# Attention units and projection passes: the second head pair's gates kept in DRAM until they are used, and a new spread of passes over the units

## The chip, the cores and the metric

The kernel runs on one core of one Trainium2 chip. The metric is the device time of one execution in microseconds (us). The core has a matrix engine (TensorE, PE; its weight loads are shown apart as PEld), VectorE (DVE), ScalarE (ACT), GpSimd (POOL) and SyncE (SP), which here only issues DMA transfers. Each engine takes its instructions in the order in which the program gives them to it.

## What is computed

A stack of four parts: a gated delta net with a pooling mixer, an MLP, a sparse attention layer and a state-space layer (S5), over 512 tokens of width 1024. The change lies in the attention layer. With 512 tokens there are 8 blocks and up to 16 may be selected, so the selected branch sees all earlier tokens, as the window branch (512) does. Per head there are three softmaxes, each with its own gate, and the sum is gated once more by silu(z):

```python
    q, kc, vc, ks, vs, kw, vw, gates, z = jnp.split(h @ w_in, splits, axis=-1)
    q = q.reshape(bsz, seq, G, R, HEAD_DIM) * (HEAD_DIM ** -0.5)
    ...
    gates = jax.nn.sigmoid(gates.astype(f32)).reshape(bsz, seq, 3, G, R)
    k_cmp = _compress(kc, cmp_idx, cmp_k_pe, cmp_k_w1, cmp_k_w2)
    v_cmp = _compress(vc, cmp_idx, cmp_v_pe, cmp_v_w1, cmp_v_w2)
    ...
        p_c = ...                        # 31 compressed keys
        p_s = _masked_softmax(s_s, m_s)  # selected blocks: all earlier tokens
        p_w = _masked_softmax(s_w, m_w)  # window: all earlier tokens
        return (gb[:, :, 0] * o_c + gb[:, :, 1] * o_s + gb[:, :, 2] * o_w)
    o = (o * jax.nn.silu(z.astype(f32))).astype(h.dtype)
    return o @ w_out
```

## The kernel before

Matrices are multiplied as three products of high and low halves. A projection of 128 output columns is one job: its weights come by DMA from SP (`load`, L97), are cut into halves by ACT and DVE (`halve`, L103 and L104), and are multiplied in 24 passes on PE (8 tiles of the model width by 3 products; `dense_steps`, L130), each 128x128 by 128x512. A job's result is then finished by its own function `done`. `steps` runs the jobs one after the other; at the top of each job it issues the loads of this job and the two behind it, cuts this one's and the next one's weights, and runs what was put off with `K.after`. A job whose condition (`ready`) is not met blocks all jobs behind it.

The attention proper is done in units. The 16 heads are taken in two pairs of groups (gp 0 and 1), each with four query tiles of 128 tokens (i 0 to 3). A tile has 9 steps: four heads of branch b=0, the compressed softmax, and four heads of branch b=1. Causality lets tile i see 128*(i+1) keys, so a unit of i=3 is about four times as long as one of i=0. Each unit has three stages: `scores` (PE products at L1189, then DVE L1197, ACT L1198, DVE L1199 to L1201, POOL L1203), three steps later `turn` (PE transposes L1247, copies L1249 and L1251), four steps later `weigh` (PE L1284). At the last `weigh` of a tile DVE multiplies the sum by the gates, `og` (L1290), and ACT and DVE split it into halves in `QS[gp]` (L232), the operand of the out projection.

PE's and SP's orders are written out by the program: `weave` puts units and passes into one sequence. After each stage a unit asks for `FILL[gp][i]/3` passes, so `FILL` is the number of passes beside one step of a tile, and while passes are ready exactly so many are put there. When none is ready the units follow one another bare; when a unit must wait for a result of a job (`seen`), passes run alone. DVE, ACT and POOL follow orders by priority, in which the units' work is rushed ahead.

When the first unit begins, six jobs are left of the layer's inputs (second keys s1 and w1, queries q4 to q7): 144 passes. Behind them stand four jobs for the second pair's gates z4 to z7 (96 passes), four double jobs for the first pair's half of the out projection (96), and the same for the second pair (96). The gates of one pair fill `sz`, one buffer that the first pair's gates use until its last `og`. So z4 to z7 have the condition `("o", 0)`: the first pair's last `og` is written. The first pair's out jobs have it too, the second pair's have `("o", 1)`. The second pair's `weigh` waits for all four gates. Other results (keys, queries) already go through `move`, a DMA from SP.

Of the kernel before, what the change touches and what calls it, by code (L numbers as in the profile page):

```python
# [9 lines left out]
F32 = mybir.dt.float32  # L10
F32R = mybir.dt.float32r
I32 = mybir.dt.int32
AF = mybir.ActivationFunctionType
ALU = mybir.AluOpType
# [946 lines left out]


LAGS = (0, 3, 4)
FILL = (8, 5, 3, 1), (8, 6.5, 4.5, 1.5)
ORDER = "v0 v1 k0 v2 v3 k1 q0 q1 k2 q2 q3 k3 s0 w0 c0 g0 z0 c1 z1 z2 c2 z3 c3 s1 w1 q4 q5 q6 q7"


def nsa(K, norms, W, cst, first, then):
# [4 lines left out]
    v, act, p = nc.vector, nc.scalar, nc.gpsimd  # L973
# [4 lines left out]
    def move(o, i, queue=nc.sync):  # L978
        queue.dma_start(o.bitcast(F32), i.bitcast(F32))

    with ExitStack() as pools:
        def pool(name, bufs, **kw):
            return pools.enter_context(tc.tile_pool(name=name, bufs=bufs, reuse_waits="tile", **kw))

        nr, nq, nw = pool("nr", 1, side="right"), pool("nq", 1), pool("nw", 2)
        na = pool("na", 2)
        nas = pool("nas", 2, space=PSUM)

        QS = [nr.tile([128, 2, 4, 4, 128], F32R, name=f"QS{gp}") for gp in range(2)]
        AT = (32, 0)  # L990
# [6 lines left out]
        sz = szb[:, 0:2048].rearrange("p (r t) -> p r t", r=4)  # L997
# [10 lines left out]
        R, held, seen, sides = {}, [], set(), []  # L1008
# [30 lines left out]
        def query(gp, r):  # L1039
# [9 lines left out]
                K.after(seen.add, ("q", gp, r))  # L1049
            return xs, done  # L1050

        def gate(gp, r):
            def done(ps):
                t = nw.tile([128, 512], F32, tag="t", name="t")
                v.scalar_tensor_tensor(t, ps, 0.5, R["rstd"], ALU.mult, ALU.mult)
                act.activation(sz[:, r, :], t, AF.Tanh)
                v.scalar_tensor_tensor(sz[:, r, :], sz[:, r, :], 1.0, t, ALU.add, ALU.mult)
                seen.add(("z", gp, r))
            return xs, done

        def values(q):
# [205 lines left out]
        def target(gp, i):  # L1267
            fresh = (gp, i) not in acc
            if fresh:
                acc[gp, i] = bank("acc", "acc")  # L1270
            return acc[gp, i], fresh

        def weigh(gp, i, b, r):

            if r % 2 == 0:
                return
            o, fresh = target(gp, i)
            for q in (r - 1, r):
                T = pend.pop((gp, i, b, q))
                for j in range(i + 1):  # L1280
                    s = slice(j * 128, j * 128 + 128)
                    for g2 in range(2):
                        c = b * 256 + (gp * 2 + g2) * 64
                        mm(o[halves[g2], q * 128:q * 128 + 128], Vt[:, j, c:c + 64], T[g2][:, s], start=fresh and (q, j) == (0, 0),  # L1284
                           stop=(b, q, j) == (1, 3, i), tile_position=(0, g2 * 64))
            if (b, r) == (1, 1):
                compressed_weigh(gp, i)
            if (b, r) == (1, 3):
                og = K.work.tile([128, 4, 128], F32, tag="acc", name="og", bufs=1)
                v.tensor_tensor(og, o.rearrange("p (r t) -> p r t", r=4), sz[:, :, i * 128:i * 128 + 128], ALU.mult)  # L1290
                K.split(QS[gp][:, 0, i], QS[gp][:, 1, i], og)
                if i == 3:
                    seen.add(("o", gp))

        def compressed_weigh(gp, i):
            T = pend.pop((gp, i))
            o, fresh = target(gp, i)
            for r in range(4):
                for g2 in range(2):
                    mm(o[halves[g2], r * 128:r * 128 + 128], Vc[:, gp * 2 + g2, r, :], T[:, g2 * 128:g2 * 128 + 128],  # L1300
                       start=False, stop=False, tile_position=(0, g2 * 64))

        SCORE, TURN, WEIGH = 0, 1, 2
        f_unit, f_comp = (scores, turn, weigh), (compressed_softmax, compressed_turn, lambda gp, i: None)

        def units():
# [4 lines left out]
            for n in range(len(items) + LAGS[2]):  # L1311
                for stage, lag in enumerate(LAGS):
# [10 lines left out]
                    if n - lag < len(items):  # L1323
                        yield FILL[at[0]][at[1]] * 0.22 / SHARE / 3, 0.0

        first[0].products = [source(0, 0)]
        first[1].products = [source(0, 1)]
        for gp in range(2):
            K.queue(W["kv"][2 + gp], [source(1, gp)])
        jobs = {"g": lambda n: K.queue(W["gates"], [branch_gates()], width=384), "v": lambda n: K.queue(W["wv"][n], [values(n)]),  # L1330
                "k": lambda n: K.queue(W["w1"][0, n], [compress(0, n)]), "c": lambda n: K.queue(W["w1"][1, n], [compress(1, n)]),
                "s": lambda n: K.queue(W["kv"][4 + n], [key(0, n)]), "w": lambda n: K.queue(W["kv"][6 + n], [key(1, n)]),
                "q": lambda n: K.queue(W["wq"][n], [query(n // 4, n % 4)]), "z": lambda n: K.queue(W["wz"][n], [gate(0, n)])}
        for job in ORDER.split():
            jobs[job[0]](int(job[1]))
        for r in range(4):
            K.queue(W["wz"][4 + r], [gate(1, r)], lambda: ("o", 0) in seen)
        for gp in range(2):
            for m in range(0, 8, 2):
                out(gp, m)  # L1340
# [642 lines left out]
def hybrid_stack(tc, W, out):  # L1983
    nc = tc.nc
    with ExitStack() as ctx:
        K = Kit(tc, ctx, W["cst"][:, C_ID:C_ID + 128])
        vec = K.consts.tile([128, VEC], F32, name="vec")
        col = {n: vec[:, a:b] for n, (a, b) in VCOLS.items()}


        ups, keys, us = [], [], []
        with tc.tile_pool(name="mix", bufs=1) as mx:
            mh = [mx.tile([128, 512], F32R, name=f"mh{k}") for k in range(8)]
            ml = [mx.tile([128, 512], F32R, name=f"ml{k}") for k in range(8)]
            V = {"conv": col["conv_w"].rearrange("p (t j) -> p t j", j=4), "pscale": col["pool_scale"],
                 "gdn": col["gdn_norm"], "alog": col["a_log"], "dtb": col["dt_bias"]}
            block1(K, (vec, W["vec"]), col["norm_mix"], W, V, mx, mh, ml, lambda: ups.extend(K.queue(W["wup"][m]) for m in range(2)))
        state = {k[2:]: v for k, v in W.items() if k.startswith("s_")}
        prepared = Prepared(K, ctx.enter_context(tc.tile_pool(name="spd", bufs=1, space=bass.MemoryType.DRAM)))
        mlp(K, W["wup"], W["wdown"], col["norm_mlp"], ups, lambda: keys.extend(K.queue(W["n_kv"][m]) for m in range(2)), prepared.steps(state, W["sc"]))  # L2000


        with tc.tile_pool(name="nc1", bufs=1) as cp:
            nc1 = cp.tile([128, 648], F32, name="nc1")
            nc.gpsimd.dma_start(nc1, W["nc1"])
            nsa(K, (col["norm_final"], col["l0_norm"]), {k[2:]: v for k, v in W.items() if k.startswith("n_")}, nc1, keys,
                lambda: us.extend(K.queue(W["s_wu"][b]) for b in range(2)))


        with ExitStack() as outer:  # L2010
            layer = S5(K, state, prepared)
            layer.begin()
            layer.run(col["l1_norm"], outer, us, (col["final_norm"], out))
# [87 lines left out]
```

## Time and profile before

| | us |
|---|---|
| median of 3 runs | 1369.45 (1366.44 to 1375.25) |
| the profiled execution | 1369.36 |
| its span, first to last instruction | 1367.6 |
| PE busy | 1295.4 |
| DVE busy | 940.3 |
| ACT busy | 548.8 |
| POOL busy | 393.3 |

The profile is of one execution. Times inside it are counted from the span's start. The units of the attention layer run from 812 to 1051. Matmuls are pipelined, so busy time on PE does not say that it worked at its full rate.

### The profile page before, as it was taken

How to read it: one execution, taken by the hardware profiler on the slowest of the kernel's cores; microseconds unless marked ns; L12 is line 12 of the kernel's file. 1: busy time of each engine (PE TensorE's matmuls, PEld its weight loads, DVE VectorE, ACT ScalarE, POOL GpSimd, SP SyncE). 2: the span in 40 equal slices, each digit the busy share in tenths (PEclk: the TensorE clock that was granted, in tenths of full speed). 3: DMA queues.
4: the chain of work that ended last, by engine and by line, in shares of the span. 5: the costliest groups of instructions: out<-in, count | busy, mean ns of one | idle time of the engine just before them, and what ended most of it. 6: DMA issues, size and time to landing. Idle time of an engine off the chain costs nothing.

```text
span 1367.6 us, 22450 instructions
## 1 busy us (share of the span) xinstructions
PE 1295.4 (95%) x8360; PEld 1041.8 (76%) x8360; DVE 940.3 (69%) x2163; ACT 548.8 (40%) x1167; POOL 393.3 (29%) x412
## 2 busy tenths in 40 slices
PE   8799989999889999999999999989988999989997
PEld 6677766877668888788888788778767777768896
DVE  7867785699954868858775667775776765634365
ACT  4323232343222323333424446753574522144364
POOL 5722442220510555443220003551353200002200
PEclk9999999999989999999999999999999999999998
DMA  5110110252233343354445845301103379753231
GB/s 189 46 48 32 32 47 29 70 167 78 64 97 102 131 151 128 138 170 144 152 128 157 207 150 140 78 1 63 47 17 122 98 205 281 206 124 108 93 109 62
DMA packets 79724, 150.83 MB, mean 110 GB/s; under 512 B 23584, under 2 KB 45520, under 8 KB 78464
## 3 DMA queue, kind: packets, MB, share of 16 engines
q1 hardware_dynamic: 69680, 126.60, 30.6%
q0 software_dynamic: 2944, 17.50, 3.8%
q10 hardware_dynamic: 6992, 5.30, 1.4%
q8 instruction: 66, 1.08, 0.3%
q14 instruction: 42, 0.34, 0.1%
HBM read 118.55 MB, written 20.35 MB: 102 GB/s over the span
## 4 chain that ended last, share of the span: by engine, by line
PE 74%; DVE 16%; issue 3%; ACT 3%; POOL 2%; DMA 1%; SPq 0%; DVEq 0%; ACTq 0%; POOLq 0%
PE ps L130 52%; DVE lo L104 3%; PE ps L1849 3%; PE pa L1189 2%; PE acc L1284 2%; PE pt L1247 2%; PE pv L1070 2%; PE py L1781 1%; PE hid L1102 1%; ACT P L1198 1%; ACT xhbuf L234 1%; PE pb L576 1%; DVE xlbuf L235 1%; DVE r L377 1%; DVE cacc L454 1%
## 5 line engine op out<-in xcount | busy, mean ns | idle before, releaser
L130 PE MATMUL ps<-xlbuf,hi 128*128 128x512 f32 x864 | 350.7, 406 | 5.2 <-DVE xlbuf L235 5.1
L130 PE MATMUL ps<-xhbuf,hi 128*128 128x512 f32 x864 | 349.7, 405 | 5.4 <-ACT xhbuf L232 4.0
L130 PE MATMUL ps<-xhbuf,lo 128*128 128x512 f32 x864 | 349.1, 404 | 0.0
L103 ACT CAST hi<-raw 128x512 fp32r<-128x512 f32 x357 | 203.0, 612 | 331.6 <-PE ps L130 249.0
L104 DVE TENSOR_TENSOR lo<-raw,hi 128x512 fp32r<-128x512 f32 x357 | 284.1, 821 | 65.1 <-ACT hi L103 64.6
L130 PEld LDWEIGHTS ps<-xhbuf,hi 128*128 128x128 f32 x864 | 164.3, 190 | 45.3 <-ACT xhbuf L232 4.4
L130 PEld LDWEIGHTS ps<-xlbuf,hi 128*128 128x128 f32 x864 | 164.1, 190 | 42.4 <-DVE xlbuf L235 7.9
L130 PEld LDWEIGHTS ps<-xhbuf,lo 128*128 128x128 f32 x864 | 164.4, 190 | 36.3 <-issue 4.8
L1203 POOL TENSOR_TENSOR P<-P,sm 128x128 f32<-128x128 f32 (+3 forms) x128 | 92.9, 747 | 211.9 <-DVE sm L1201 173.6
L130 PE MATMUL ps<-hh,lo 128*128 128x512 f32 x256 | 102.2, 399 | 6.1 <-DVE lo L104 6.1
L130 PE MATMUL ps<-hh,hi 128*128 128x512 f32 x256 | 101.0, 395 | 4.5 <-ACT hi L103 4.5
L130 PE MATMUL ps<-hl,hi 128*128 128x512 f32 x256 | 101.0, 395 | 0.0
L1198 ACT ACTIVATE P<-P,nm 128x128 f32<-128x128 f32 (+3 forms) x128 | 71.8, 562 | 57.6 <-DVE nm L1197 50.1
L1610 POOL TENSOR_TENSOR F<-keep 128x1024 f32<-128x1024 f32 x16 | 36.1, 2255 | 126.2 <-PE pt L1636 110.0
L1197 DVE CUSTOM_DVE_ANT_0 P<-pa,nc 128x128 f32<-128x128 f32 (+3 forms) x128 | 59.1, 485 | 10.4 <-PE pa L1189 9.5
L130 PEld LDWEIGHTS ps<-hh,lo 128*128 128x128 f32 x256 | 48.7, 190 | 19.2 <-DVE lo L104 8.9
L130 PEld LDWEIGHTS ps<-hh,hi 128*128 128x128 f32 x256 | 48.6, 190 | 15.4 <-ACT hi L103 5.7
L1247 PE MATMUL pt<-ident,P 128*128 128x128 f32 x320 | 49.0, 279 | 8.8 <-ACT T L1251 5.3
L130 PEld LDWEIGHTS ps<-hl,hi 128*128 128x128 f32 x256 | 48.6, 190 | 10.5 <-DVE hl L232 0.3
L386 DVE TENSOR_TENSOR hbuf<-hbuf,ps 128x512 f32<-128x512 f32 x32 | 21.9, 685 | 47.6 <-PE ps L130 47.6
L1247 PEld LDWEIGHTS pt<-ident,P 128*128 128x128 f32 x320 | 38.1, 142 | 20.6 <-issue 9.5
L1610 POOL TENSOR_TENSOR V<-keep 128x1152 f32<-128x1152 f32 x16 | 39.9, 2496 | 42.6 <-DMA DM<-V 42.0
(553 smaller groups left out, 2356.9 us busy)
## 6 DMA issues: line engine op xcount, KB each, us to landing
raw<-in_wup_dram SPq DMA_DIRECT2D x32, 512.0 KB, 3.6
raw<-in_wdown_dram SPq DMA_DIRECT2D x32, 512.0 KB, 3.6
made<-DM POOLq DMA_DIRECT2D x8, 1472.0 KB, 9.2
raw<-in_win_dram SPq DMA_DIRECT2D x19, 512.0 KB, 3.4
raw<-in_s_wglu_dram SPq DMA_DIRECT2D x16, 512.0 KB, 3.5
DM<-V SPq DMA_DIRECT2D x8, 576.0 KB, 3.0
DM<-Wt SPq DMA_DIRECT2D x8, 512.0 KB, 2.9
raw<-in_n_kv_dram SPq DMA_DIRECT2D x8, 512.0 KB, 3.7
```

The lines of the kernel that those rows point to most:

```text
L103: self.nc.scalar.copy(hi[:, s], raw[:, s])
L104: self.nc.vector.tensor_tensor(lo[:, s], raw[:, s], hi[:, s].bitcast(F32), ALU.subtract)
L130: mm(ps, w[:, s], xs[k][x], start=k == 0 and n == 0, stop=k == kt - 1 and n == 2)
L1070: mm(R["v"][i], x[k][:, i * 128:i * 128 + 128], w[:, s], start=k == 0 and n == 0, stop=k == 7 and n == 2)
L1189: mm(pa[g2][:, 0:lead + nk], QS[gp][:, g2, i, r, :], keys[b][:, gp * 2 + g2, key0:AT[b] + nk], start=n == 0, stop=n == 1)
L1197: v.tensor_tensor_reduce(P[g2][:, 0:nk], pa[g2][:, lead:lead + nk], pos[:, 512 - nk:512], -slope, 3e38, ALU.add, ALU.min, nm[:, g2:g2 + 1])
L1198: act.activation(P[g2][:, 0:nk], P[g2][:, 0:nk], AF.Exp, scale=-1.0, bias=nm[:, g2:g2 + 1], accum_out=sm[:, g2:g2 + 1])
L1203: p.tensor_tensor(P[g2][:, 0:nk], P[g2][:, 0:nk], sm[:, g2:g2 + 1].to_broadcast([128, nk]), ALU.mult)
L1247: nc.tensor.transpose(pt[:, s], P[g2][:, s], ident)
L1284: mm(o[halves[g2], q * 128:q * 128 + 128], Vt[:, j, c:c + 64], T[g2][:, s], start=fresh and (q, j) == (0, 0), stop=(b, q, j) == (1, 3, i), ...
L1610: eng.tensor_tensor(o, self.S[f][:, js, b * 8:b * 8 + 8].rearrange("p j x -> p x j")[:, :, :, None].to_broadcast([128, 8, n, 16]), m[:, :, ...
L1849: nc.tensor.matmul(banks[m][:, 0:256], w[:, s], os[k][x][:, a * 256:a * 256 + 256], start=k == 0 and n == 0, stop=k == 7 and n == 2)
```

## The change

The second pair's gates lose their condition. Each is built in a working tile and written to a DRAM tile `szd[r]` by a DMA from SP. When all four are there and the first pair's last `og` is written, `fetch_gates` loads the four into `sz`. `FILL` gets other numbers.

```diff
 LAGS = (0, 3, 4)
-FILL = (8, 5, 3, 1), (8, 6.5, 4.5, 1.5)
+FILL = (7, 6, 6, 5.5), (3, 2.5, 2.5, 2)
...
+        nd = pool("nd", 1, space=bass.MemoryType.DRAM)
+        szd = [nd.tile([128, 512], F32, name=f"szd{r}") for r in range(4)]
...
+        def fetch_gates():
+            if seen >= {("o", 0)} | {("zd", r) for r in range(4)} and ("z", 1, 0) not in seen:
+                for r in range(4):
+                    move(sz[:, r, :], szd[r])
+                    seen.add(("z", 1, r))
+
         def gate(gp, r):
             def done(ps):
                 t = nw.tile([128, 512], F32, tag="t", name="t")
                 v.scalar_tensor_tensor(t, ps, 0.5, R["rstd"], ALU.mult, ALU.mult)
-                act.activation(sz[:, r, :], t, AF.Tanh)
-                v.scalar_tensor_tensor(sz[:, r, :], sz[:, r, :], 1.0, t, ALU.add, ALU.mult)
-                seen.add(("z", gp, r))
+                z = nw.tile([128, 512], F32, tag="t", name="z") if gp else sz[:, r, :]
+                act.activation(z, t, AF.Tanh)
+                v.scalar_tensor_tensor(z, z, 1.0, t, ALU.add, ALU.mult)
+                if gp:
+
+                    K.after(move, szd[r], z)
+                    K.after(seen.add, ("zd", r))
+                    K.after(fetch_gates)
+                else:
+                    seen.add(("z", gp, r))
             return xs, done
...
                 if i == 3:
                     seen.add(("o", gp))
+                    fetch_gates()
...
         for r in range(4):
-            K.queue(W["wz"][4 + r], [gate(1, r)], lambda: ("o", 0) in seen)
+            K.queue(W["wz"][4 + r], [gate(1, r)])
```

## Rows read from the trace of the kernel before

**Rows 1.** The page, busy time of each engine, its share of the span and instructions

```profile
PE 1295.4 (95%) x8360; PEld 1041.8 (76%) x8360; DVE 940.3 (69%) x2163; ACT 548.8 (40%) x1167; POOL 393.3 (29%) x412
```

**Rows 2.** Windows by stage: us, busy us of each engine (instructions), clock, DMA share, GB/s

```profile
812.00:838.20 26.20, 26.20 (x155) 21.41 (x155) 20.34 (x100) 14.30 (x55) 6.41 (x15) 1.00 0.53 135
838.20:862.20 24.00, 24.00 (x177) 19.71 (x176) 19.50 (x90) 16.91 (x55) 9.67 (x16) 1.00 0.48 118
862.20:886.60 24.40, 22.28 (x190) 18.30 (x190) 19.83 (x86) 18.63 (x56) 12.80 (x17) 1.00 0.38 88
886.60:917.10 30.50, 27.39 (x239) 21.94 (x237) 23.06 (x83) 16.66 (x43) 16.40 (x18) 0.94 0.01 2
917.10:929.20 12.10, 10.94 (x125) 9.40 (x124) 9.72 (x57) 7.47 (x27) 6.46 (x11) 1.00 0.01 1
929.20:950.60 21.40, 21.40 (x96) 17.68 (x96) 9.19 (x18) 5.98 (x12) 1.37 (x3) 1.00 0.22 71
950.60:963.70 13.10, 13.10 (x80) 10.36 (x79) 8.99 (x37) 7.17 (x27) 2.57 (x6) 1.00 0.17 57
963.70:989.60 25.90, 25.90 (x185) 21.05 (x184) 18.77 (x87) 14.90 (x52) 10.86 (x17) 1.00 0.16 57
989.60:1010.70 21.10, 19.32 (x174) 15.38 (x172) 17.93 (x83) 16.10 (x49) 11.77 (x16) 1.00 0.08 26
1010.70:1041.80 31.10, 26.01 (x237) 20.56 (x236) 23.66 (x88) 19.04 (x49) 16.52 (x18) 1.00 0.01 1
1041.80:1052.40 10.60, 8.03 (x105) 6.90 (x105) 3.88 (x9) 3.23 (x7) 5.96 (x13) 1.00 0.41 145
```

**Rows 3.** The same windows, L130 alone: us, PE busy (passes), PEld busy, clock, DMA

```profile
812.00:838.20 26.20, 21.17 (x75) 12.80 (x75) 1.00 0.53 135
838.20:862.20 24.00, 16.53 (x53) 8.52 (x52) 1.00 0.48 118
862.20:886.60 24.40, 6.31 (x18) 2.82 (x17) 1.00 0.38 88
886.60:917.10 30.50, 0.00 (x0) 0.00 (x0) 0.94 0.01 2
929.20:950.60 21.40, 21.40 (x94) 17.43 (x94) 1.00 0.22 71
950.60:963.70 13.10, 11.13 (x40) 6.27 (x38) 1.00 0.17 57
963.70:989.60 25.90, 18.41 (x61) 9.81 (x60) 1.00 0.16 57
989.60:1010.70 21.10, 0.18 (x1) 0.00 (x0) 1.00 0.08 26
```

**Rows 4.** Waits from 876 to 929: who waited for whom, us in total, times, longest

```profile
ACT P L1198 <- DVE nm L1197: 13.8, 10, 3.5
POOL P L1203 <- DVE sm L1201: 11.9, 8, 3.6
```

**Rows 5.** Timeline of PE: start, length, instruction [idle before <-releaser]

```profile
904.41 0.50 PE L1189 MATMUL pa<-K,QS 128*128 128x512 f32 x1 [1.93 <-DVE cm L1215]
...
1052.38 0.50 PE L130 MATMUL ps<-QS,hi 128*128 128x512 f32 x1 [1.44 <-ACT QS L232]
```

**Rows 6.** DMA issues from 800 to 1060: queue, count, KB each, median us to landing

```profile
made<-DM POOLq DMA_DIRECT2D x3, 1472.0 KB, 8.8
raw<-in_n_wout_dram SPq DMA_DIRECT2D x8, 512.0 KB, 3.5
...
QS<-hi SPq DMA_DIRECT2D x8, 128.0 KB, 2.5
```

**Rows 7.** Groups by line from 800 to 1060: busy us, mean ns | idle before, releasers

```profile
L104 DVE TENSOR_TENSOR lo<-raw,hi 128x512 fp32r<-128x512 f32 x38 | 26.6, 725 | 0.2 <-ACT hi L103 0.2
...
L1057 DVE SCALAR_TENSOR_TENSOR sz<-sz,t 128x512 f32<-128x512 f32 x7 | 4.8, 686 | 0.0
L1055 DVE SCALAR_TENSOR_TENSOR t<-ps,rstd 128x512 f32<-128x512 f32 x6 | 4.2, 692 | 16.8 <-PE ps L130 16.8
```

## Prediction

> **What bounds the kernel now.** I read the page's shares first: PE is busy for 95% of the span and DVE for 69% [rows 1]. That is a mean over stages, so next come windows cut at the starts of the attention tiles, first all engines [rows 2], then the passes alone [rows 3]. The reader should see four kinds of stretch between 812 and 1052.4, which together last 240.4 us. (a) With passes beside them (tiles i=0 and i=1 of both pairs), PE is busy without a gap; DVE is busy 0.69 to 0.81 of the time. (b) The first pair's passes run out in tile i=2: 18 are left there and none in i=3, where PE idles 30.5-27.39 = 3.1 us and the others are not full either. (c) From 929.2 to 950.6 some 94 passes run alone, the second pair's gates; DVE is busy for 9.19 of 21.40 us. (d) From 989.6 on the second pair is bare again: 1 pass in i=2, PE idle 1.8, 5.1 and 2.6 us in the last three windows. In (b) and (d) the wait that ends last is that of a chain: ACT waits for DVE's minimum, POOL for DVE's sums [rows 4], and PE, in its fixed order, for what they make. So the work is there, but unevenly laid: passes without units in (c), units without passes in (b) and (d).
>
> **How many passes stand where.** The four gate jobs are 4x24 = 96 passes. With them free, 144+96 = 240 passes can stand beside the first pair. New FILL asks for 9x(7+6+6+5.5) = 220, a few more because later stages lag by 3 and 4 steps: 63 in i=0, 56.3 in i=1, 54 in i=2, 50.7 in i=3, together 224, and the 16 left in the four steps in which the first pair's last stages overlap the second pair's first. That is 240 when the first pair's last og comes, so stretch (c) vanishes. The second pair then has its 96 out passes: some 15 in the rest of i=0, 23.7, 22.7 and 19.2 in i=1 to 3, 4.7 in the tail, and 11 left over behind the last unit.
>
> **Prices.** A pass alone takes 21.40/94 = 0.228 us [rows 3]; I take 0.23 beside units. Units at PE's full rate: i=0 26.2-75x0.23 = 8.95 us; i=1 24.0-53x0.23 = 11.8 and, in the second pair, 25.9-61x0.23 = 11.9, two readings of the same thing [rows 2, 3]. Tiles i=2 and i=3 were never seen filled. I scale their weight-load time: i=1's units load for 19.71-8.52 = 11.2 us and take 11.8, a ratio of 1.055. Then i=2 is (18.30-2.82)x1.055 = 16.3, i=3 20.56x1.055 = 21.7 (the second pair's, since the first's holds a drop of the clock), the four overlapping steps 9.40x1.055 = 9.7.
>
> **First pair, 812 to 950.6, 138.6 us before.** PE's demand: i=0 8.95+63x0.23 = 23.4; i=1 11.8+56.3x0.23 = 24.8; i=2 16.3+54x0.23 = 28.7; i=3 21.7+50.7x0.23 = 33.4; overlapping steps 9.7+16x0.23 = 13.4. To this I add 2 us in i=3 for the compressed softmax, before which PE stood 1.93 us for DVE [rows 5]; 1.5 us after the last og, because the first out pass now comes right behind it and must wait for the split as at the end (1.44 us [rows 5]), where before the gates' passes hid it; and 2 us because DVE comes near its own limit: its work here is 20.34+19.50+19.83+23.06+9.72+9.19 = 101.6 us, the same after, and in 129 us that is a share of 0.79, where the fullest window shows 17.93/21.10 = 0.85 [rows 2]. Sum 129.2, a gain of 9.4.
>
> **Second pair, 950.6 to 1052.4, 101.8 us before.** Rest of i=0: 13.1-40x0.23 = 3.9 or 4.09x1.055 = 4.3 of units, 4.1, and 15x0.23: 7.6. i=1: PE 11.9+23.7x0.23 = 17.4; DVE does 18.77 less 37 passes at 9.19/94 = 0.1, 15.1, which at 0.85 is 17.7: 17.9. i=2: PE 16.3+22.7x0.23 = 21.5; DVE 17.93+2.2 = 20.1, at 0.85 23.7; between them 22.8. i=3: PE 21.7+4.4 = 26.1, but bare it already took 31.1 by its chain, so the passes mostly fill idle time: 32. Tail: 9 us to the last product plus 1.1, and the 11 left-over passes (2.5 us), which cover the wait of 1.44 us for the last split: 12.1 after a little overlap, for 10.6. Sum 92.4, a gain of 9.4.
>
> **Costs that I set at nothing.** DVE and ACT make the gates with the same three instructions (L1055 692 ns, L1057 686 ns [rows 7]), only earlier; that is in DVE's 101.6 us. Four writes and four loads of 256 KB are new. The nearest rows are 128 KB in 2.5 us and 512 KB in 3.5 us [rows 6], so about 3 us each. They issue from SP. Each write waits there for its gate; behind it stands the next job's weight load, which has 24 passes and several units of time. The four loads into sz wait for the last og and the last write; behind them stands the third or fourth out job's weight load, needed 48 passes later. The gates are first read at the og of the second pair's i=0, nine steps on; nine steps of i=0 last over 15 us, two transfers 6 us. If that cover were gone, og would be late, and PE behind it at the next tile's weigh, since the sum has a single bank. The layer behind (S5) starts its large loads (1472 KB in 8.8 us [rows 6]) after the last unit, and moves with it. The second pair's 96 out passes at the end stay bare, as before.
>
> **Clock.** Over 886.6 to 917.1 the granted clock was 0.94 [rows 2], so about 2x0.06x30.5 = 3.7 us at 1.2 GHz, which costs at most 1.8 us; filled stretches show 1.00. That gain is inside the price of i=3 above.
>
> **A rule on reading PE.** By busy time PE idles only 15.8 us in all the windows of [rows 2], so hiding passes could seem to bring no more than that. The Trainium skill (Perfetto Trace Analysis, Identifying the Most-Contended Engine) says that matmul busy share is no good measure of what PE has left, because pipelined instructions overlap, and asks for the weight-load share instead. The rows agree that the two differ: weight loads fill 17.68 of 21.40 us (0.83) in the stretch of passes alone, 0.82 in i=1, and only 20.56 of 31.10 (0.66) in the bare i=3. By busy time the best sum would be 1369.4-15.8 = 1353.6; by weight loads, 182.7 us at 0.82 is 222.8, a gain of 17.6, 1351.8. Nothing in my sum hangs on it.
>
> **Sum.** 9.4+9.4 = 18.8 us off the profiled execution's 1369.36 is 1350.6; I say 1351. That execution stands 0.1 us from the median of the three runs.
>
> **Bounds.** If PE's demand alone counted: 123.7 in the first part and, with 7.6+17.4+21.5+26.1+10.9 = 83.5, in the second, a gain of 33.2: 1336. If no moved pass hid in idle time, the first part is 23.4+24.8+32.7+42.2+15.8+1.5 = 140.4 (bare tiles plus their passes at 0.23) and the second 7.6+17.9+26.3+35.5+12.5 = 99.8, together 240.2: no gain.
>
> **Rivals.** (1) DVE and the chain cap it. Filled or bare, the longest tiles show DVE at 23.06/30.5 = 0.76; if no better is to be had over the whole, the parts last 101.6/0.76 = 133.7 and 73.2/0.76 = 96.3 us, a gain of 10.4: 1359. For it: i=3 is where most passes go. Against: 0.81 to 0.85 in i=1 and i=2 with passes. (2) The passes add. PE's order is fixed and a unit's scores are followed by passes before its transposes, so each step gets longer by its passes: 1369, no change. For it: the chain of [rows 4]. Against: 53 passes beside i=1 left PE without a gap. (3) PE near its best, everything else hidden: 1340. For it: PE is full in (a); against: DVE would have to reach 101.6/124 = 0.82 and stay there. (4) Slower: the weights' halves come late. Their DVE work (L104, 725 ns, two per job [rows 7]) is not rushed; where DVE is full, it queues behind units, PE stops at the job's first pass and with it every unit. From i=2 on there are (54+50.7+16+96)/24 = 9 job boundaries; at two units of DVE backlog (2x23.06/9 = 5.1 us) each, 46 us: 1397. It decides against the change from 18.8/9 = 2.1 us per boundary. Against: at 0.81 in i=1 PE shows no gap at all [rows 2].
>
> **Chances.** Forecast 1351 (its own range 1343 to 1356): 0.56. PE near its best, below 1343: 0.09. Cap by DVE: 0.18. Passes add: 0.10. Halves late: 0.07. A measurement of this kernel tells about 1%, 13.7 us, from no change: faster by more (forecast and the best case) 0.65, within 0.28 (cap and adding), slower 0.07. The range 1340 to 1364 leaves out adding, late halves and a part of the best case.
>
> **What would show it.** Right: no stretch of some 20 us with only passes; passes in every tile, about 50 beside the first pair's i=3; i=2 and i=3 of the first pair near 29 and 36 to 37 us, the second pair's i=1 to i=3 near 18, 23 and 32; the second pair's first out product some 19 us earlier than 1052.4; no wait of og for sz; an unchanged distance from there to the end. Wrong: DVE's share at 0.76 with PE waiting for the minima (rival 1), i=3 of the first pair at 42 us (rival 2), PE waiting for halves at job starts (rival 4), or a gain that is spent again in S5.

## The result and the profile after

The changed kernel takes 1359.37 us (median of 6 runs, 1357.94 to 1362.83), the kernel before 1370.59 us over its 6 runs (1366.44 to 1375.25); the ratio is 0.9926, 95% interval 0.9908 to 0.9944. That is 11.2 us, 0.8%: inside the predicted range of 1340 to 1364, but short of the 1351 that was forecast, and less than the 1% that the chances called faster. The whole interval lies below 1, so the gain is small but real. The profiled execution took 1357.94 us, 11.4 less than the profiled one before. Of these 11.4 us 10.6 lie in the attention stage, and 1.6 ahead of it (810.7 for 812.3 us, 17.1 for 27.3 us of them at half clock), in code that the change does not touch; behind the stage 0.8 are lost.

Lines moved down by some 15 in the new kernel: scores are at L1204 (before L1189), transposes L1262, weighing L1299, `og` L1305. These are the windows of the new kernel cut at the same places as [rows 2] (us, busy us of PE, PEld, DVE, ACT and POOL with the instructions, clock, DMA share, GB/s): the first pair's tiles i=0 to i=3, the steps that overlap, the switch to the second pair, the rest of its i=0, its i=1 to i=3, and the tail up to the second pair's first out pass.

```profile
810.70:835.50 24.80, 24.35 (x144) 19.40 (x143) 19.66 (x98) 13.71 (x52) 6.41 (x15) 1.00 0.47 122
835.50:860.50 25.00, 25.00 (x181) 20.27 (x181) 18.66 (x88) 16.01 (x55) 9.93 (x17) 1.00 0.57 134
860.50:890.30 29.80, 29.80 (x227) 25.20 (x227) 24.96 (x92) 20.48 (x58) 16.01 (x17) 1.00 0.32 81
890.30:927.20 36.90, 36.20 (x288) 30.10 (x287) 28.33 (x96) 21.42 (x54) 16.88 (x17) 1.00 0.14 47
927.20:938.40 11.20, 10.39 (x99) 8.92 (x98) 5.81 (x39) 5.11 (x19) 4.07 (x7) 1.00 0.11 40
938.40:947.00 8.60, 5.63 (x47) 4.34 (x46) 6.45 (x25) 4.25 (x13) 2.91 (x5) 0.85 0.36 121
947.00:954.40 7.40, 7.40 (x53) 5.98 (x52) 4.25 (x27) 3.36 (x17) 1.77 (x5) 0.94 0.30 111
954.40:974.20 19.80, 18.60 (x150) 14.69 (x150) 15.74 (x87) 14.78 (x54) 8.99 (x17) 1.00 0.08 28
974.20:996.80 22.60, 22.60 (x196) 19.65 (x195) 19.41 (x86) 17.21 (x53) 13.84 (x18) 1.00 0.08 25
996.80:1028.70 31.90, 29.34 (x256) 24.15 (x254) 25.41 (x89) 19.36 (x51) 17.97 (x19) 1.00 0.06 18
1028.70:1040.00 11.30, 10.70 (x116) 9.08 (x117) 4.39 (x10) 3.41 (x7) 4.85 (x12) 1.00 0.43 149
```

The reader should see that the stretch of passes alone is gone, that the first pair's i=2 and i=3 last 29.8 and 36.9 us for 24.4 and 30.5 before [rows 2], and that the second pair's i=1 to i=3 last 19.8, 22.6 and 31.9. The passes alone (L130) show where the 54 and 51 asked for went; before there were 18 and none [rows 3]:

```profile
860.50:890.30 29.80, 17.01 (x55) 9.12 (x54) 1.00 0.32 81
890.30:927.20 36.90, 16.59 (x52) 8.76 (x51) 1.00 0.14 47
...
974.20:996.80 22.60, 9.23 (x24) 3.88 (x23) 1.00 0.08 25
996.80:1028.70 31.90, 7.96 (x20) 3.20 (x19) 1.00 0.06 18
```

So 52 more passes cost the first pair's i=3 6.4 us, 0.12 us each, and 20 cost the second's 0.8 us, 0.04 each, where a pass alone takes 0.228. They do hide, though the first figure flatters them: the bare i=3 held 3.4 us at half clock, worth up to 1.7 us, and without it a pass costs up to 0.16 us.

One window does not fit: 938.4 to 947.0, 8.6 us in which PE is busy for 5.63. PE there (timeline: start, length, instruction, idle before and who ended it):

```profile
939.26 1.97 PE L1299 MATMUL acc<-T,Vt 128*64 128x128 f32 x32
943.79 0.49 PE L130 MATMUL ps<-QS,hi 128*128 128x512 f32 x1 [2.56 <-ACT QS L232]
944.69 0.80 PE L130 MATMUL ps<-QS,hi 128*128 128x512 f32 x1 [0.40 <-DVE QS L232]
```

and DVE, which had first to serve the halves of weights:

```profile
941.41 0.68 DVE L104 TENSOR_TENSOR lo<-raw,hi 128x512 fp32r<-128x512 f32 x1
...
942.42 0.67 DVE L1305 TENSOR_TENSOR og<-acc,sz 128x512 f32<-128x512 f32 x1
...
943.14 0.68 DVE L104 TENSOR_TENSOR lo<-raw,hi 128x512 fp32r<-128x512 f32 x1
943.86 0.77 DVE L232 TENSOR_TENSOR QS<-og,QS 128x512 fp32r<-128x512 f32 x1
```

The last `weigh` of the first pair ends at 941.23. The next thing in PE's order is the first pair's first out pass, which needs the split of the last `og`. `og` itself starts only at 942.42, because DVE is at a weight half and at the softmaxes of the second pair's first units; PE stands 2.56 and then 0.40 us, with the second pair's units behind it. Then the granted clock falls (windows of 2 us, all engines):

```profile
940.00:942.00 2.00, 1.23 (x24) 0.98 (x18) 1.93 (x7) 1.72 (x8) 0.00 (x0) 1.00 0.16 50
942.00:944.00 2.00, 0.21 (x1) 0.19 (x1) 2.00 (x9) 0.62 (x1) 0.60 (x1) 1.00 0.25 93
944.00:946.00 2.00, 1.60 (x6) 1.01 (x5) 0.92 (x2) 0.00 (x0) 1.51 (x3) 0.61 0.82 264
946.00:948.00 2.00, 2.00 (x9) 1.81 (x8) 0.30 (x2) 0.43 (x2) 0.00 (x0) 0.54 0.86 311
```

### The profile page after: what moved, and what is told of

Same layout as the page of the kernel before. It is cut to its first block, busy times and chain, and to the rows that moved or that the text cites. A ratio compares the mean times of both kernels' runs of the same rounds, so it can differ in the third digit from the quotient of the medians.

```text
span 1356.2 us, 22477 instructions
## 1 busy us (share of the span) xinstructions
PE 1287.1 (95%) x8360; PEld 1037.6 (77%) x8360; DVE 938.2 (69%) x2163; ACT 549.4 (41%) x1167; POOL 396.2 (29%) x412
## 4 chain that ended last, share of the span: by engine, by line
PE 69%; DVE 17%; DMA 4%; issue 4%; ACT 3%; POOL 2%; SPq 1%; DVEq 0%; ACTq 0%; POOLq 0%
PE ps L130 48%; DVE lo L104 4%; PE ps L1865 3%; PE pa L1204 3%; PE acc L1299 2%; PE pt L1262 2%; DMA Uc<-D 2%; PE pv L1085 2%; DMA T<-DK 1%; DVE xlbuf L235 1%; ACT P L1213 1%; DVE r L377 1%; PE pb L576 1%; DVE cacc L454 1%; PE hid L1117 1%
## 5 line engine op out<-in xcount | busy, mean ns | idle before, releaser
L130 PE MATMUL ps<-xlbuf,hi 128*128 128x512 f32 x864 | 351.5, 407 | 6.3 <-DVE xlbuf L235 6.3
L130 PE MATMUL ps<-xhbuf,hi 128*128 128x512 f32 x864 | 349.9, 405 | 5.8 <-ACT xhbuf L232 4.0
L130 PE MATMUL ps<-xhbuf,lo 128*128 128x512 f32 x864 | 349.0, 404 | 0.1
L130 PEld LDWEIGHTS ps<-xhbuf,hi 128*128 128x128 f32 x864 | 163.7, 190 | 45.8 <-issue 6.7
L130 PEld LDWEIGHTS ps<-xlbuf,hi 128*128 128x128 f32 x864 | 164.1, 190 | 42.5 <-DVE xlbuf L235 9.0
L130 PEld LDWEIGHTS ps<-xhbuf,lo 128*128 128x128 f32 x864 | 164.1, 190 | 35.4 <-issue 4.5
L1218 POOL TENSOR_TENSOR P<-P,sm 128x128 f32<-128x128 f32 (+3 forms) x128 | 96.5, 775 | 199.2 <-DVE sm L1216 139.3
L130 PE MATMUL ps<-hh,lo 128*128 128x512 f32 x256 | 101.9, 398 | 6.1 <-DVE lo L104 6.1
L130 PE MATMUL ps<-hh,hi 128*128 128x512 f32 x256 | 100.9, 394 | 5.3 <-ACT hi L103 5.3
L130 PE MATMUL ps<-hl,hi 128*128 128x512 f32 x256 | 100.6, 393 | 0.1
L130 PEld LDWEIGHTS ps<-hh,lo 128*128 128x128 f32 x256 | 48.4, 189 | 19.1 <-DVE lo L104 8.8
L130 PEld LDWEIGHTS ps<-hh,hi 128*128 128x128 f32 x256 | 48.6, 190 | 15.8 <-ACT hi L103 6.1
L130 PEld LDWEIGHTS ps<-hl,hi 128*128 128x128 f32 x256 | 48.6, 190 | 10.8 <-DVE hl L232 0.6
L130 PE MATMUL ps<-QS,hi 128*128 128x512 f32 x128 | 47.6, 430 | 3.0 <-ACT QS L232 2.6
L1262 PE MATMUL pt<-ident,P 128*128 128x128 f32 x320 | 47.0, 275 | 3.5 <-ACT T L1266 1.9
```

The costliest lines, as they stand in the source:

```text
L130: mm(ps, w[:, s], xs[k][x], start=k == 0 and n == 0, stop=k == kt - 1 and n == 2)
L1218: p.tensor_tensor(P[g2][:, 0:nk], P[g2][:, 0:nk], sm[:, g2:g2 + 1].to_broadcast([128, nk]), ALU.mult)
L1262: nc.tensor.transpose(pt[:, s], P[g2][:, s], ident)
```

## The experiments

For every kernel the same stage is measured in its profiled execution: from the first `scores` of the units to the first out pass of the second pair. In it all kernels do the same 336 passes and the same units. "Half" is the time in which TensorE was granted 1.2 GHz, from the clock records of the trace. "Rest" is from the end of the stage to the end of the span, where all programs do the same work. Each ratio is against runs of the kernel before on the same chip (medians 1370.59 for after, 1368.97 for the next four, 1370.01 for the four behind them, 1369.30 for the last three).

| kernel | median us | ratio to before, 95% interval | stage us (half) | rest us (half) |
|---|---|---|---|---|
| before | 1370.59 | | 240.1 (3.4) | 315.2 (18.7) |
| after | 1359.37 | 0.9926, 0.9908 to 0.9944 | 229.5 (3.4) | 316.0 (19.2) |
| fill_only | 1366.49 | 0.9981, 0.9971 to 0.9991 | 235.9 (0) | 316.3 (22.4) |
| gates_only | 1376.47 | 1.0063, 1.0045 to 1.0081 | 245.3 (17.1) | 318.0 (20.3) |
| cover | 1359.59 | 0.9938, 0.9916 to 0.9959 | 230.6 (3.4) | 313.1 (10.7) |
| twohops | 1364.38 | 0.9960, 0.9950 to 0.9971 | 234.2 (10.2) | 313.8 (15.1) |
| gates_dve | 1372.79 | 1.0014, 0.9999 to 1.0029 | 241.7 (13.7) | 317.4 (23.2) |
| after_dve | 1359.10 | 0.9920, 0.9902 to 0.9939 | 230.0 (3.4) | 319.6 (26.1) |
| cover_dve | 1359.20 | 0.9919, 0.9902 to 0.9936 | 230.4 (3.4) | 314.7 (15.5) |
| defer | 1359.18 | 0.9912, 0.9894 to 0.9930 | 226.8 (0) | 318.7 (26.1) |
| gates_order | 1372.29 | 1.0018, 1.0002 to 1.0034 | 239.1 (6.8) | 316.8 (22.6) |
| softmax_fill_order | 1352.97 | 0.9869, 0.9851 to 0.9888 | 225.0 (3.4) | 313.6 (15.7) |
| defer_cover_order | 1356.15 | 0.9899, 0.9885 to 0.9913 | 228.4 (6.8) | 314.5 (16.6) |

The stage and the rest are read from one execution each, while the medians are of 4 to 10 runs; so a difference of a microsecond or two in the rest need not be the kernel's. Some of the differences below are time at half clock; it is counted at half of itself, the most that it can cost where the clock is 1.2 instead of 2.4 GHz. The prediction put the stage at 129.2+92.4 = 221.6 us; the kernel after has 229.5. The first question was which part brings the gain, the second where the missing 7.9 us are.

**fill_only.** The kernel before with the new numbers alone.

```diff
-FILL = (8, 5, 3, 1), (8, 6.5, 4.5, 1.5)
+FILL = (7, 6, 6, 5.5), (3, 2.5, 2.5, 2)
```

> Kernel before with the new FILL alone: gates still wait for the first pair's last og. Theory A (the gain lies in the second pair, where the out passes are spread evenly, and the first pair gains little because the switch between the pairs gives it back): the first pair keeps its bare stretch and the 21 us of gate passes alone, about 138 us; the second pair falls from 101.8 to about 94 us; 8 us less than before, 1361 to 1363. Theory B (the gates in DRAM are what gains, since only they let passes stand beside the first pair's long tiles): no change, 1368 to 1372.

It gained 2.5 us (0.2%), the stage 4.2, of which up to 1.7 us are the 3.4 us at half clock that this execution does not have. Theory A was right on the place and wrong on the size: from the first pair's first out pass on the stage takes 96.0 us for 101.2, ahead of it 139.9 for 138.8. The second pair's i=1 fell from 25.9 to 18.5 us, but i=2 rose from 21.1 to 23.2 and i=3 with the tail, to the last `weigh`, from 40.2 to 42.7: the passes that no longer stand in i=1 stand in tiles that were bare. The difference is small; before, i=1 was full and lost nothing.

**gates_only.** The kernel after with the old numbers.

```diff
-FILL = (7, 6, 6, 5.5), (3, 2.5, 2.5, 2)
+FILL = (8, 5, 3, 1), (8, 6.5, 4.5, 1.5)
```

> Kernel after with the old FILL: the gate passes may stand beside the first pair, but only some 3 and 1 per step in its long tiles, so about 56 of them are left at the switch and run alone there (13 us). Theory A: first pair about 134 us instead of 138.6, second pair as before, 101.8; 5 us less than before, 1364 to 1366; and no wait for the split of the last og, since the left-over passes cover it. Theory B: most of the whole gain, 8 to 11 us, 1359 to 1362.

Neither theory: it is 0.6% slower than before. The first pair's i=3, with 13 passes, takes 39.2 us, more than with 52 in the kernel after, and 8.7 more than bare. The timeline of POOL and of PE:

```profile
914.03 4.05 POOL L1218 TENSOR_TENSOR P<-P,sm 128x512 f32<-128x512 f32 x4 [2.95 <-ACT P L1213]
918.04 0.61 POOL L1250 TENSOR_TENSOR sc<-sc,cm 128x256 f32<-128x256 f32 x1
```

```profile
918.71 0.69 PE L1274 MATMUL pt<-ident,sc 128*128 128x128 f32 x2 [7.05 <-POOL sc L1250]
```

PE waits 7.05 us for the product of the compressed softmax, L1250, which POOL reaches only behind four products of later units. POOL's order in the programs explains a part of it: in i=3 the kernels before and after have 8 unit products, the compressed one, and 8 more; gates_only has 14, the compressed one, and 2. POOL's order, which follows priorities, came out differently here. The product's last factor (L1249) is ready on DVE at 914.19, and POOL starts the product at 918.04: 3.9 of the 7.05 us are POOL's order, most of what is left is DVE's. That the stall came from such orders and not from the passes is what the next two runs test. The clock fell 3.1 us into the stall and was at half for 10.2 us, which is up to 5.1 of the tile's 39.2 us. The switch gives 7.3 us back, and the second pair's i=3 with what follows takes 45.1 us for 41.7; there the clock was at half for 6.8 us.

**gates_dve.** gates_only with that product on DVE.

```diff
-            p.tensor_tensor(s8, s8, m8[:, :, None].to_broadcast([128, 8, 32]), ALU.mult)
+            v.tensor_tensor(s8, s8, m8[:, :, None].to_broadcast([128, 8, 32]), ALU.mult)
```

> gates_only with one instruction of the compressed softmax, the product at L1250, on VectorE instead of GpSimd. Theory E (gates_only was slow because this product stood in GpSimd's queue behind four units' products, so PE waited 7.05 us for it and then ran 10 us at half clock): wait and low clock vanish, first pair's i=3 from 39.2 to about 31 us, 8 to 12 us less than gates_only, 1364 to 1369. Theory F (one pass per stage beside the longest units stretches their chain): i=3 stays near 39 us, 1374 to 1378.

i=3 fell to 35.7 us and the whole by 3.7 us, less than theory E said. PE's wait at the same transposes is 3.36 us now, for DVE, and the clock is at half for 6.8 us of that tile: the wait got shorter, it did not vanish.

**gates_order.** gates_only with POOL's two kinds of product held in the order of the program, 8, the compressed one, 8.

```diff
-                p.tensor_tensor(P[g2][:, 0:nk], ...)
+                tc.keep_in_program_order(p.tensor_tensor(P[g2][:, 0:nk], ...))
...
-            p.tensor_tensor(s8, s8, ...)
+            tc.keep_in_program_order(p.tensor_tensor(s8, s8, ...))
```

> gates_only, with GpSimd's products of the units (L1218) and of the compressed softmax (L1250) held in the order of the program: 8 unit products before the compressed one in the first pair's i=3, where gates_only has 14. Theory E (that order made gates_only slow): PE's wait of 7.05 us for L1250 vanishes, the first pair's i=3 falls from 39.2 to 31 to 33 us, total 1364 to 1368. Theory F (passes in ones and twos beside the longest units slow their chain): i=3 stays at 36 us or more, 1372 to 1377.

```profile
914.99 0.61 POOL L1250 TENSOR_TENSOR sc<-sc,cm 128x256 f32<-128x256 f32 x1 [9.87 <-DVE sm L1215]
```

```profile
915.66 0.44 PE L1274 MATMUL pt<-ident,sc 128*128 128x128 f32 x2 [2.85 <-POOL sc L1250]
```

i=3 falls to 33.7 us, nearly theory E's 31 to 33; POOL's order, with the clock that fell in its stall (10.2 us at half, 3.4 here), was worth 5.5 of the 8.7 us by which gates_only's i=3 exceeds the bare one. PE still waits 2.85 us, since POOL itself waits 9.87 us for DVE. The total fell only to 1372.3, above E's 1364 to 1368, so E explains the stall and not the time. The stage is 239.1, 1.0 under before. With the old numbers some 50 gate passes are still left to run alone at the switch (12.1 us), and the second pair is bare in i=2 and i=3 as before. With the old numbers the gates in DRAM bring nothing that shows in the time, though a wait of PE for POOL is left in this test.

**cover.** Fewer passes beside the first pair's long tiles, so that some 12 gate passes stand between the last `og` and the first out pass.

```diff
-FILL = (7, 6, 6, 5.5), (3, 2.5, 2.5, 2)
+FILL = (7, 6, 5.5, 4.5), (3, 2.5, 2.5, 2)
```

> Kernel after with FILL (7, 6, 5.5, 4.5) for the first pair: some 12 gate passes are left when the last og comes, and stand between it and the first out pass. Theory A (in the kernel after PE waits at the switch for the split of the last og, 2.56 us, then runs 3.4 us at half clock): the wait and the drop of the clock behind it vanish, 3 to 5 us less than the kernel after, 1354 to 1356. Theory C (the missing gain is the price of the passes beside long tiles): first pair's i=2 and i=3 get about 2.6 us shorter by 11 passes, the switch longer by the same, no change, 1358 to 1360.

The wait for the split is gone as theory A said, and the time is that of the kernel after, as C said, but not for C's reason. PE now waits one step earlier, in the overlapping steps:

```profile
932.06 0.63 PE L1262 MATMUL pt<-ident,P 128*128 128x128 f32 x4 [0.52 <-ACT T L1266]
933.89 0.87 PE L1262 MATMUL pt<-ident,P 128*128 128x128 f32 x4 [1.21 <-DVE sm L1215]
...
935.12 3.13 PE L1299 MATMUL acc<-T,Vt 128*64 128x128 f32 x32
```

The last line is the second-last `weigh` of the first pair, which the kernel after does at full clock:

```profile
932.77 1.97 PE L1299 MATMUL acc<-T,Vt 128*64 128x128 f32 x32
```

In cover the clock was at half for 3.4 us from 934.1. PE waits at the same two places in the kernel after, but for 0.24 and 0.57 us; that fewer passes let PE catch up with DVE's backlog of the i=3 units fits, and is not shown apart. By tile, against the kernel after: the first pair's i=2 and i=3 are 2.2 us shorter, the switch up to the second pair's i=1 is 0.3 longer with 9 more passes in it, and the second pair's i=3 with what follows is 2.6 longer. So most of what was won is lost in the last tile. There PE waits for the compressed product:

```profile
1026.64 0.61 POOL L1250 TENSOR_TENSOR sc<-sc,cm 128x256 f32<-128x256 f32 x1 [2.26 <-DVE sm L1216]
```

```profile
1027.31 0.44 PE L1274 MATMUL pt<-ident,sc 128*128 128x128 f32 x2 [2.22 <-POOL sc L1250]
```

POOL's order has 10 products before it instead of 8, but that is not the reason, since POOL stands idle for 2.26 us and then starts 0.15 us behind L1249. It is DVE's order: DVE's last three steps before the product (L1247 to L1249) are spread over 2.8 us between the units' work, where the kernel after has them within 0.6.

**cover_dve and after_dve.** The edit of gates_dve in cover and in the kernel after.

> cover with the same product on VectorE. Theory E: the 2.2 us that PE waited for it in the second pair's i=3 vanish and the switch stays clean, 1355 to 1358. Rival G (what is taken away at one place comes back at another, because the orders of VectorE, ScalarE and GpSimd are planned anew for every program): no change against cover, 1358 to 1361.

> Kernel after with the same product on VectorE. There no wait of PE for it was seen, and VectorE gets 0.4 us more per tile. Theory E: no change, 1358 to 1361. Rival (VectorE is the limit in the filled tiles): 2 to 4 us slower than the kernel after.

Both stayed where they were, 1359.2 and 1359.1. But cover_dve does not test rival G, since PE's wait did not go away; it is nearly as long as in cover, for the other engine, and the second pair's last tile up to its last `weigh` takes 43.1 us for 43.3:

```profile
1027.09 0.41 PE L1274 MATMUL pt<-ident,sc 128*128 128x128 f32 x2 [2.02 <-DVE sc L1250]
```

So here the engine of the product was not the cause of the wait: its last factor, L1249, starts on DVE at 1026.34 here and at 1026.35 in cover. DVE's extra 0.4 us per tile costs nothing in after_dve.

**twohops.** Each gate goes to `sz`, back to DRAM and to `sz` once more.

```diff
                     move(sz[:, r, :], szd[r])
+                    move(szd[r], sz[:, r, :])
+                    move(sz[:, r, :], szd[r])
```

> Kernel after with two more transfers per gate: szd to sz, sz back to szd, szd to sz, one after the other, eight transfers more, about 6 us later in sz. Theory A (the trip through DRAM is covered by the second pair's first tile): no change against the kernel after, 1358 to 1361, sz landing before its first og. Theory D (the gates' arrival or SP's queue holds the second pair up, and that is where the missing gain is): 4 to 7 us slower than the kernel after, 1363 to 1367.

It is 5 us slower than after, as D said, but the six us of the expectation were wrong: SP waits for each transfer before it issues the next one, and the last load leaves SP at 967.96, not some 6 us after the first.

```profile
944.18 0.33 SPq L979 DMA_DIRECT2D sz<-szd  x1
...
967.96 0.32 SPq L979 DMA_DIRECT2D sz<-szd  x1
```

```profile
971.65 1.20 PE L1301 MATMUL acc<-T,Vt 128*64 128x128 f32 x16 [3.07 <-DVE og L1307]
```

`og` of the second pair's i=0 then waits, and PE 3.07 us at the next tile's `weigh`, the chain that the prediction named for this case. Of the 4.7 us by which the stage is longer, 3.3 are in that tile, which also holds 3.4 us at half clock; the other 1.4 are at the switch, where the same waits as in the kernel after (2.57 and 0.40 us) are followed by 6.8 us at half clock for 3.4. So the run does not test D at 6 us but measures the cover. In the kernel after the last load is issued at 944.5, lands within 4.3 us, and `og` reads `sz` at 963.5: about 15 us of slack. The trip through DRAM costs nothing there.

**defer.** The kernel after, with the first pair's out jobs released two steps later; the gates are fetched as soon as before.

```diff
-            K.queue(src, [add(m), add(m + 1)], lambda: ("o", gp) in seen)
+            K.queue(src, [add(m), add(m + 1)], lambda: (("out" if gp == 0 else "o"), gp) in seen)
...
                         f[stage](*at)
+                    if stage == 2 and n == 41:
+                        seen.add(("out", 0))
```

> Kernel after, but the first pair's out passes are released two steps later, so that units of the second pair and not out passes follow the last og in PE's order. Theory A (the switch costs some 5 us, because out passes wait for the split and hold the units behind them): PE's wait for the split vanishes, 2 to 4 us less than the kernel after, 1355 to 1358. Rival (without passes PE has as little to do there, the units wait for VectorE): no change, 1358 to 1361.

PE's order at the switch holds units now, and no wait for the split:

```profile
943.82 0.44 PE L1262 MATMUL pt<-ident,P 128*128 128x128 f32 x2
944.01 0.31 PE L1204 MATMUL pa<-K,QS 128*128 128x128 f32 x1
...
945.81 0.66 PE L1299 MATMUL acc<-T,Vt 128*64 128x128 f32 x8 [0.66 <-DVE og L1305]
946.46 0.50 PE L130 MATMUL ps<-QS,hi 128*128 128x512 f32 x1
```

From the second pair's first scores to its i=1 it takes 23.1 us where the kernel after has 27.2, i=1 takes 18.2 for 19.8, and none of the stage runs at half clock: theory A's mechanism. But the stage is only 2.7 us shorter. 3.0 us come back in the second pair's i=3 with what follows, where 39 passes stand for 32, since seven of the passes that were put off at the switch are left over at the end (some 1.6 us at 0.23). Of the 2.7 us up to 1.7 are the missing half clock. The total is the same, 1359.18: the rival's number. In the two profiled executions, 1360.67 us for 1357.94, the 2.7 us are lost again ahead of the stage (813.4 for 810.7 us) and once more behind it (318.7 for 316.0). Over all six runs the mean granted clock is the same, 0.982 for both kernels, and a difference of one or two microseconds is below what six runs each can tell.

**softmax_fill_order and defer_cover_order.** Both are defer with POOL's order held. The first moves six passes behind the compressed softmax's products of i=3, where PE waits for DVE (1.93 us in the first pair's before [rows 5]; in the kernel after 0.70 there and 1.66 in the second pair's); the second takes cover's numbers.

```diff
-FILL = (7, 6, 6, 5.5), (3, 2.5, 2.5, 2)
+FILL = (7, 6, 6, 4.8), (3, 2.5, 2.5, 1.6)
...
-                        yield FILL[at[0]][at[1]] * 0.22 / SHARE / 3, 0.0
+                        extra = 18 if f is f_comp and stage == 0 and at[1] == 3 else 0
+                        yield (FILL[at[0]][at[1]] + extra) * 0.22 / SHARE / 3, 0.0
```

```diff
-FILL = (7, 6, 6, 5.5), (3, 2.5, 2.5, 2)
+FILL = (7, 6, 5.5, 4.5), (3, 3, 2.5, 2)
```

> defer, with GpSimd's order held as in gates_order, and six passes moved behind the compressed softmax's products of i=3 in either pair, where PE waited 1.66 us for VectorE; FILL of i=3 4.8 and 1.6 to keep their sum. Theory A and E together: units to the second pair's out passes 223 to 226 us (kernel after 229.5), total 1353 to 1357. Rival H (a gain in this stage does not reach the time, since the half clock outside it takes it back): stage 3 to 6 us shorter, total 1358 to 1361.

> defer with cover's FILL for the first pair, (3, 3, 2.5, 2) for the second, and GpSimd's order held. Some 12 gate passes fill the switch. Theory A: switch as clean as in defer, stage 225 to 228 us, total 1354 to 1358. Rival H: stage as forecast, total 1358 to 1361.

softmax_fill_order is the best kernel of the study: 1352.97 us, 1.3% under before (0.9851 to 0.9888), 6.4 us under the kernel after, the stage in theory A's range and the time at the lower end of its range; rival H's 1358 to 1361 is not met. Some of the 6.4 us may be the clock, whose mean is 0.984 over its runs for 0.982. The first pair's i=3 has no gap left:

```profile
890.70:926.90 36.20, 36.20 (x289) 30.45 (x289) 28.22 (x96) 21.08 (x52) 17.58 (x17) 1.00 0.15 48
```

The stage is 4.5 us shorter than after's and 1.8 shorter than defer's, 0.7 of it in the first pair's i=3 and 2.1 in the second pair's last tile, less some 1 in between. It differs from defer by two edits, the held order and the moved passes, and their shares were not measured apart. Of the 9.2 us between the profiled executions of the two 1.8 lie in the stage, 2.3 ahead of it and 5.1 behind. defer_cover_order shows cover's wait in the overlapping steps again (one of these steps takes 8.9 us in both, 6.4 in the kernel after): its stage, 228.4, just misses its range of 225 to 228 and is 3.4 us longer than softmax_fill_order's. Its time, 1356.15, is in theory A's range.

**What the rest of the time does.** Behind the stage all programs do the same work, yet take 313.1 to 319.6 us. Two rows of windows that end the span, of defer and of softmax_fill_order:

```profile
1040.20:1358.90 318.70, 300.77 (x1955) 248.08 (x1953) 170.04 (x279) 125.70 (x206) 31.27 (x26) 0.96 0.49 146
```

```profile
1036.10:1349.70 313.60, 296.13 (x1955) 244.93 (x1954) 169.96 (x279) 125.75 (x206) 31.30 (x26) 0.97 0.51 148
```

Take half of the time at half clock away from the rest, and 315.2-9.4 = 305.8 for before, 306.4 for after, 305.7 for defer and 305.8 for softmax_fill_order remain; over all 13 kernels 305.1 to 307.9, where the rests as they are spread over 6.5 us. So the differences there are mostly the clock's. Whether a program has much or little time at half clock there because of what it does, or only in the execution that was profiled, was not tried and stays open: among the six runs of the kernel after alone the mean granted clock goes from 0.979 to 0.985, 57 to 41 us at half over the whole span. Between the executions shown here it is worth up to (26.1-10.7)/2 = 7.7 us, more than the 4.5 us by which the stage was shortened after the first result, and enough to hide them.

## Why the prediction was right and where it was not

- **The bound and the direction: right; the size: about half.** The passes alone are gone, the passes stand beside the long tiles and hide there. The stage gained 10.6 us of the 18.8 that were forecast, and the second pair's first out product came 12.1 us earlier, not 19. The time lies in the range of 1340 to 1364, but above the forecast's own 1343 to 1356; it is the width of the range, which took in the cap by DVE, that holds it.
- **The middle tiles: the sums held, one price did not.** 29.8 us for i=2 and 36.9 for i=3 of the first pair (expected near 29, and 36 to 37), 22.6 and 31.9 for the second pair's (22.8 and 32). For i=2 the price scaled from weight loads by 1.055 came out well. For the first pair's i=3 the total is right partly by luck: the sum had 33.4 us of PE's work and 2 us of wait for the compressed softmax, but PE was busy for 36.20 us and waited 0.70. In softmax_fill_order the tile takes 36.2 us without any gap. So the units of i=3 beside passes cost some 2.8 us more than their price, and the wait that was added did not come.
- **Both parts of the change are needed: not separated beforehand.** New numbers alone 2.5 us; the gates alone are slower, and with POOL's order held no faster than before; together 11.2.
- **The switch: the term that was mis-sized.** The overlapping steps and the wait for the split were put at 13.4+1.5 = 14.9 us and took 11.2+8.6 = 19.8. The step named the right wait but took its size from the end of the stage, 1.44 us [rows 5], where DVE has nothing else to do; here DVE is busy for 1.93 and 2.00 of 2 us around it, and `og` comes 1.2 us late. 2.56+0.40 us of wait and 3.4 us at half clock behind it were the price, with the units queued behind the out pass on PE. To the second pair's i=1 the kernel after takes 27.2 us where the sum had 14.9+7.6 = 22.5: 4.7 of the missing 7.9 us. defer, which takes that pass away, has 23.1 there, with seven passes fewer, some 1.6 us; so about 2.5 of the 4.7 are shown by an experiment to hang on the pass, and the others are read from the waits and the clock of the kernel after alone. About 1.9 us more are in the second pair's i=1 (19.8 for 17.9, with a wait of 0.73 us for POOL), and 1.4 in the first pair's i=0, which had 66 passes and 24.8 us for 63 and 23.4. The other windows nearly cancel.
- **The costs at nothing: right.** `sz` landed some 15 us before it was read, and no wait of `og` for it appears. The layer behind moved along; from the first out pass to the end it is 316.0 us for 315.2, with the clock's half-time difference in it.
- **The half clock: too small.** It was taken as a gain inside the price of i=3. The one drop in the stage did vanish there, and another came at the switch, 3.4 us each. That the time at half clock differs by more than this outside the stage, 10.2 us between the two profiled executions ahead of it alone, was not seen.
- **Rival 1 (DVE caps at 0.76, 1359) met the number.** DVE's share of the stage is 173.28/229.5 = 0.755. That the number fits is chance, since as a reason for the whole it fails: in 927.2 to 938.4 DVE is busy 5.81 of 11.2 us, i=3 of the first pair is PE's (36.20 of 36.90), and softmax_fill_order has the same DVE work in 225.0 us. In a smaller place it holds: at the switch PE waited for DVE, and in cover as well.
- **Rival 2 (passes add): no;** they cost 0.12 to 0.16 and 0.04 us each in i=3. **Rival 4 (halves late): not at job starts,** but a kin of it is real: halves ahead of `og` in DVE's queue, 0.68 us of the 1.2 by which it is late. **Rival 3** (PE near its best, everything hidden, 1340): no; PE waited at the switch.
- **The chance for more than 1%, 0.65, was too high.** The sum added the likeliest value of each place, and nothing in it stood for a handover that comes out worse.
- **Not foreseen at all:** that the orders of POOL and DVE come out differently for each program, and that this can cost 5.5 us in one tile (gates_only against gates_order).

## What to carry to other kernels

When free-floating work is spread beside a pipeline of units, the sums for the middle held here within some 2 us a tile; look at the handover, at which instruction stands next in PE's fixed order when the last unit of a group is done, and let it be one that needs nothing of that unit. Size a wait by what the waited-for engine has in its queue at that place, not by the same wait at a quiet one. And when a small edit of the order makes a kernel slower, compare the queues of the other engines instruction by instruction before blaming the edit, and after the cure look whether the wait is gone or has only changed its engine (cover_dve).

## What the runs showed of the hardware

The granted clock fell to 1.2 GHz for 3.4 us at 944.4, in the second of two waits of PE of 2.56 and 0.40 us (kernel after), and at 934.1, 0.2 us behind waits of 0.52 and 1.21 us (cover); in gates_only it fell 3.1 us into a wait of 7.05 us, for 10.2 us. A wait of 1.66 us at 1015.3 in the kernel after had no such drop behind it, so the length of the wait alone does not tell. The same kind of product, 32 of them at L1299, took 1.97 us at the one clock and 3.13 us across the drop. Behind the stage, where the work is the same, the time at half clock was 10.7 to 26.1 us from one profiled execution to another; half of it taken away, the time there agrees within 2.8 us instead of 6.5. A load of 256 KB from DRAM into `sz` took 3.4 us (median of four, 2.6 to 4.3), a write 2.0 us (median of four), while a chain of twelve such transfers that wait for each other on SP stretched over 24 us.
